# One block of linear attention on one core: where queries of the second token tile meet the first tile, and how a column of 2048 numbers is written

## The chip, the core and the metric

The kernel runs on one NeuronCore of a Trainium2 chip. Five engines work side by side and wait for each other through semaphores: TensorE (PE in the rows, with its weight loads as PEld), VectorE (DVE), ScalarE (ACT), GpSimd (POOL) and SyncE (SP), which issues most transfers. The metric is device time in microseconds; lower is better.

## The reference, cut to what matters

One transformer block for 256 tokens of width 2048, with 256 context tokens. Everything is float32. Two branches (window attention and a gated linear recurrence, "hgrn") are merged and projected. The change touches the recurrence, for each of 16 heads in both directions, and the output gate:

```
f = lbf + (1.0 - lbf) * jax.nn.sigmoid(z)          # forget gate; k = 1 - f
S_new = exp(G_end)[..., None] * S + einsum('bhsk,bhsv->bhkv', k * exp(G_end - G), v)
o     = einsum('bhtk,bhkv->bhtv', q * exp(G), S) + (the same chunk's keys, causal)
...
shift, scale, gate = jnp.split(silu(c) @ w_ada + b_ada, 3)
h = h + gate * merge_and_project(...)
```

A query therefore sees all earlier tokens either one by one, as keys and values with the decay between, or summed up in a state of 128 x 128 per head and direction.

## The kernel before, in words

The time goes into projections: 2048 x 19456 weights, streamed from HBM as `raw`, split by ACT (`wh`, L76) and by DVE (`wl`, L77) into two parts, and multiplied in three passes (L83, L84, L85). One chunk of weights is 24 matmuls of 512 columns; `wh` and `wl` have three buffers each, so ACT refills one as soon as the last matmul that reads it ends, three chunks ahead of its use.

The recurrence runs in eight steps, two heads each (`pair`, numbered here first to eighth). The order of PE's instructions is written out by hand: `pair` is a generator that issues some work and yields a number, and `weave` then lets that many units (1 unit = one chunk of 24 x 512 columns) of the next pair's projections (`inputs`) be issued before it goes on. The order on DVE and ACT is not written by hand; a scheduler sets it when the kernel is built, with the steps L76 and L77 at a higher priority.

A pair holds keys and queries of both directions in `A` (keys in A[0] and A[3], queries in A[2] and A[1]), the state from the context in `S` (a part of the tile `so`), and 256 tokens as two tiles of 128. It builds the products of queries and keys within a tile level by level (blocks of 1, 2, 4 to 64 tokens, `level`, L562, into the banks `al`); `grow` (L616) multiplies decays into `A` after each level; `keep` and `spread` copy the products into `AT`, the first half of the tile `X2` (printed `X` in the rows), through the piece `near` of its second half. Then three steps end a pair:

- four products across the two tiles, queries of the later against keys of the earlier (L677, L678, bank `a5`), which ACT copies into the second half of `AT` (L682); `grow(128)` multiplies the other tile's total decay into the queries (L610, L613);
- 1.5 units of filler;
- the outputs `ob`: for each tile and head four matmuls, own tile (L694), other tile (L696), and the two states (L697, L698).

Another generator, `gates`, sums up the output gate beside all this, on DVE, in four groups. `gate_end` turns a group with four PE transposes (`tqg`, L202), DVE reduces it (L204) and adds it into the column `gcol` (L206). After the fourth group POOL issues one transfer that writes `gcol`, 128 partitions of 16 numbers, to HBM in the order of 16 rows of 128 (L778); it is read back near the end. Next in POOL's order are the transfers of the bias rows `bb` (L465).

Of the kernel before, what the change touches and what calls it, by code (L numbers as in the profile page):

```python
# [7 lines left out]
F32 = mybir.dt.float32  # L8
F32R = mybir.dt.float32r
U8 = mybir.dt.uint8  # L10
AF = mybir.ActivationFunctionType
ALU = mybir.AluOpType
PSUM = bass.MemoryType.PSUM

P = 128
D = 2048
T = 256
KT = D // P
HD = 128
# [19 lines left out]
def block_kernel(ctx: ExitStack, tc: tile.TileContext, x, c, cx, c_ctx, w_ada, b_ada, norm_gain, w_in,  # L39
                 b_merge, lb_f, lb_b, hg_gain, w_oh, sink, w_oa, w_out, fin_gain, cst, msk, out):  # L40
    nc = tc.nc
    pe, act, dve, pool = nc.tensor, nc.scalar, nc.vector, nc.gpsimd

    def pl(name, bufs=1, **kw):
        return tc.tile_pool(name=name, bufs=bufs, **kw)
# [5 lines left out]
    base = ctx.enter_context(pl("base"))  # L51
    wp = ctx.enter_context(pl("wp"))
    pj = ctx.enter_context(pl("pj", 4, space=PSUM))
    ps = ctx.enter_context(pl("ps", 1, space=PSUM))
# [106 lines left out]
    ident = cs[:, K_ID: K_ID + P]  # L161
# [26 lines left out]
    def gate_chunk(acc, g, k0):  # L188

        wr = wload(w_ada, k0 * P, 2, (4096 + 512 * g,), 512)[1][:, 0]  # L190
        for j in range(2):
            cc = cg[:, k0 + j: k0 + j + 1]
            if k0 + j == 0:
                dve.tensor_scalar(acc, wr[:, j, :], cc, None, op0=ALU.mult)
            else:
                dve.scalar_tensor_tensor(acc, wr[:, j, :], cc, acc, op0=ALU.mult, op1=ALU.add)
# [20 lines left out]
    gcol = few.tile([P, KT], F32, name="gcol")  # L217
    gate_rows = dram.tile([KT, P], F32, name="gate_rows")

    FIRST = (("F0", 2), ("F1", 1), ("F0", 2))  # L220
    with pl("st", reuse_waits="tile") as st:
# [12 lines left out]
        with tc.high_priority(3 * PRIO):  # L234
# [8 lines left out]
            tp = ps.tile([P, 512], F32, tag="tp", name="tp")  # L243
# [11 lines left out]
        tp = ps.tile([P, 512], F32, tag="tp", name="tp")  # L255
# [220 lines left out]
    def pair(g, p, grp, F, banks_q):  # L476

        h0 = 4 * g + 2 * p
        v, vc, _ = grp

        A = hp.tile([P, 4, 512], F32, tag="A", name="A")
        X2 = hp.tile([P, 2048], F32, tag="X2", name="X2")
# [3 lines left out]
        Kmt = hp.tile([P, 2, 512], F32, tag="Km", name="Kmt")  # L486

        def v3(ap):
            return ap.rearrange("p (h t) -> p h t", h=2)
# [56 lines left out]
        def level(al, c0, b):  # L546

            n = 64 if b == 64 else 32
            for a in range(4):
                for g in range(4):  # L550
                    s0 = a * P + 32 * g
                    t0 = a * P + (32 * (g ^ 1) if b == 32 else 64 * (1 - g // 2) if b == 64 else 32 * g)
                    o = al[32 * g: 32 * g + 32, c0 + a * n: c0 + a * n + n]
                    if b == 0:
                        ky, mv = ksum[:, s0: s0 + 32], qT[:, t0: t0 + 32]
                    elif b in qslot:
                        ky, mv = cut(kslot[b], s0, 32), cut(qslot[b], t0, n)
                    else:
                        ky = cut(kslot[b], s0, 32)
                        o = o.rearrange("p (n two b) -> p n two b", two=2, b=b)  # L560
                        mv = mix(1, 1, t0, n, b)
                    pe.matmul(o, ky, mv, start=True, stop=True, tile_position=(0, 32 * g))  # L562

        def keep(al, c0, b):

            if b == 64:
                for c in range(2):
                    hf = slice(64 * c, 64 * c + 64)
                    act.activation(AT[hf, 0:4, 64 * (1 - c): 64 * (2 - c)],
                                   al[hf, c0: c0 + 256].rearrange("p (a b) -> p a b", a=4), AF.Copy)  # L570
# [8 lines left out]
        def spread():  # L579
            for g in range(4):  # L580
                rows = slice(32 * g, 32 * g + 32)
                for z in range(2):
                    c0 = 32 * (g ^ z)
                    act.activation(AT[rows, 0:4, c0: c0 + 32], near[rows, :, 32 * z: 32 * z + 32], AF.Copy)

        tots = {}

        def grow(b):

            n2 = 512 // (2 * b)  # L590
            if b == 1:
                even = [F[d][:, :, 0:T].rearrange("p h (n two) -> p h n two", two=2)[:, :, :, 0] for d in range(2)]
                odd = [F[d][:, :, 0:T].rearrange("p h (n two) -> p h n two", two=2)[:, :, :, 1] for d in range(2)]
            else:
                tv = tots[b].rearrange("p d (n two) -> p d n two", two=2)
                even, odd = tv[:, :, :, 0], tv[:, :, :, 1]
            toff = 1024 - 2 * 512 // b
            Tn = TT[:, toff: toff + 2 * n2].rearrange("p (d n) -> p d n", d=2)
            if b == 1:
                for d in range(2):  # L600
                    for a, par, f in ((d, 0, odd[d]), (2 + d, 1, even[d])):
                        av = v3(A[:, a, :]).rearrange("p h (n two) -> p h n two", two=2)[:, :, :, par]
                        dve.tensor_tensor(av, av, f, op=ALU.mult)
                    dve.tensor_tensor(v3(Tn[:, d, :]), even[d], odd[d], op=ALU.mult)
            else:
                for a0, par, f in ((0, 0, odd), (2, 1, even)):
                    av = A[:, a0: a0 + 2, :].rearrange("p a (n two b) -> p a n two b", two=2, b=b)[:, :, :, par, :]
                    if b == 128 and a0 == 0:

                        dve.tensor_tensor(av[:, 1], av[:, 1], f[:, 1].unsqueeze(2).to_broadcast([P, n2, b]),  # L610
                                          op=ALU.mult)
                    elif b == 128:
                        dve.tensor_tensor(av[:, 0], av[:, 0], f[:, 0].unsqueeze(2).to_broadcast([P, n2, b]),  # L613
                                          op=ALU.mult)
                    else:
                        dve.tensor_tensor(av, av, f.unsqueeze(3).to_broadcast([P, 2, n2, b]), op=ALU.mult)  # L616
                if b < 128:
                    dve.tensor_tensor(Tn, even, odd, op=ALU.mult)
            tots[2 * b] = Tn

        AT = X2[:, :1024].rearrange("p (a t) -> p a t", a=8)

        near = X2[:, 512:768].rearrange("p (a b) -> p a b", a=4)
        TT = X2[:, 1024:]
# [21 lines left out]
        S = so[:, 0, :].rearrange("p (d h v) -> p d h v", d=2, h=2)  # L646
        sb = ps.tile([P, 512], F32, tag="o", name="sb")
        for d in range(2):
            for i in range(2):
                o = sb[:, (2 * d + i) * HD: (2 * d + i + 1) * HD]  # L650
                for s in range(2):
                    pe.matmul(o, wT[:, 4 * d + 2 * i + s, :], vc[:, s, (2 * p + i) * HD: (2 * p + i + 1) * HD],  # L652
                              start=s == 0, stop=s == 1)
        act.activation(so[:, 0, :], sb, AF.Copy, scale=-1.0)

        grow(1)
        copies(2)
        grow(2)
        copies(4)
        yield 1.5  # L660
# [3 lines left out]
        for b in (4, 8, 16, 32):  # L664
            grow(b)
            copies(2 * b)
# [4 lines left out]
        a3, a4 = al_bank(), al_bank()  # L671
        for al, c0, b in ((a3, 0, 8), (a3, P, 16), (a3, 2 * P, 32), (a4, 0, 64)):
            level(al, c0, b)
        a5 = ps.tile([P, 512], F32, tag="o", name="al")
        for i in range(2):
            t0, t1 = slice(i * T, i * T + P), slice(i * T + P, (i + 1) * T)
            pe.matmul(a5[:, 2 * i * P: (2 * i + 1) * P], A[:, 0, t0], A[:, 2, t1], start=True, stop=True)  # L677
            pe.matmul(a5[:, (2 * i + 1) * P: (2 * i + 2) * P], A[:, 3, t1], A[:, 1, t0], start=True, stop=True)  # L678
        for al, c0, b in ((a3, 0, 8), (a3, P, 16), (a3, 2 * P, 32), (a4, 0, 64)):
            keep(al, c0, b)  # L680
        spread()
        act.activation(AT[:, 4:8, :], a5.rearrange("p (a b) -> p a b", a=4), AF.Copy)  # L682
        grow(128)
        yield 1.5


        ob = ps.tile([P, 2, 2, HD], F32, tag="o", name="ob")
        for t in range(2):
            tq = slice(t * P, (t + 1) * P)
            for i in range(2):  # L690
                o = ob[:, t, i, :]
                hv = slice((2 * p + i) * HD, (2 * p + i + 1) * HD)
                ht = slice(i * T + t * P, i * T + (t + 1) * P)
                pe.matmul(o, AT[:, 2 * i + t, :], v[:, t, hv], start=True, stop=False)  # L694

                pe.matmul(o, AT[:, 4 + 2 * i + (1 - t), :], v[:, 1 - t, hv], start=False, stop=False)  # L696
                pe.matmul(o, A[:, 2, ht], S[:, 0, i, :], start=False, stop=False)  # L697
                pe.matmul(o, A[:, 1, ht], S[:, 1, i, :], start=False, stop=True)  # L698
        srs = few.tile([P, 8], F32, tag="ss", name="ss", bufs=2)
        ss, rs = srs[:, :4], srs[:, 4:]  # L700
        ot = so[:, 1, :].rearrange("p (t h v) -> p t h v", t=2, h=2)
# [4 lines left out]
        for t in range(2):  # L706
            for i in range(2):
                dve.scalar_tensor_tensor(ot[:, t, i, :], ob[:, t, i, :], rs[:, 2 * t + i: 2 * t + i + 1],
                                         grp[2][:, t, (2 * p + i) * HD: (2 * p + i + 1) * HD],
                                         op0=ALU.mult, op1=ALU.mult)  # L710
# [59 lines left out]
    def gates():  # L770

        for g in range(4):
            for k0 in range(0, KT, 2):
                gate_chunk(accT[:, 0, :], g, k0)
                yield
            gate_end(accT[:, 0, :], g)

        nc.gpsimd.dma_start(gate_rows.rearrange("k p -> p k"), gcol)  # L778
        while True:
            yield  # L780

# [312 lines left out]
    for k0 in range(0, KT, 4):  # L1094
        h, lo = wchunk(w_out, k0 * P, 4, D - 512, 256)
# [15 lines left out]
    for t in range(2):  # L1111
# [7 lines left out]
        for c0, c1, on_act in ((0, 512, True), (512, 1024, False), (1024, 1536, True), (1536, D, False)):  # L1119
# [3 lines left out]
            else:  # L1123
                e = min(c1, D - 256)
                dve.tensor_scalar(xv[t][:, c0: e], xv[t][:, c0: e], rs, None, op0=ALU.mult)
                if e < c1:
                    dve.scalar_tensor_tensor(xv[t][:, e: c1], xv[t][:, e: c1], rs, fg[1][:, e - 1024: c1 - 1024],
                                             op0=ALU.mult, op1=ALU.mult)
# [54 lines left out]
```

## Time and profile before

| what | value |
|---|---|
| three timed runs | 1647.79, 1649.04, 1650.03 us; median 1649.04 us |
| the profiled execution | 1650.36 us, of which 1648.6 us from the first to the last instruction |
| PE busy | 1621.8 us, 98% of the span |
| DVE, ACT, POOL busy | 57%, 46%, 2% |
| TensorE's granted clock, mean | 0.994 |

The profile gives for each instruction its start, its length and what ended the idle time before it; matmuls overlap, so the distance between starts, not the length of one, is what PE pays for each.

### The profile page before, as it was taken

What the parts mean: (1) busy time and instruction counts of PE and PEld (TensorE: products, weight loads), DVE (VectorE), ACT (ScalarE), POOL (GpSimd) and SP (SyncE); (2) the same over time, 40 slices, a digit from 0 to 9 for tenths busy, and PEclk for the clock granted to TensorE, in tenths of its full rate; (3) what the DMA queues carried; (4) which work ended last, traced back from release to release, by engine and by line L of the source; (5) the groups of instructions that cost most, each with busy time, mean ns of one, the idle gap of its engine ahead of it and who ended that gap; (6) DMA issues with size and microseconds to landing.
All of it is one profiled execution on the core that took longest, in us unless ns stands there. A gap on an engine that the chain in (4) does not pass through costs nothing.

```text
span 1648.6 us, 24835 instructions
## 1 busy us (share of the span) xinstructions
PE 1621.8 (98%) x9913; PEld 1336.3 (81%) x9913; DVE 934.4 (57%) x1447; ACT 763.4 (46%) x1199; POOL 31.9 (2%) x88
## 2 busy tenths in 40 slices
PE   7999999999999999999899999999999999999998
PEld 4558888888888888888788888888888888788887
DVE  4444567546664466645457555334677676555665
ACT  4333454424543345424356443223576777444443
POOL 2000000000000000000000000000000000000000
PEclk9999999999999999999899999999999999999999
DMA  9993444346333553436335566424545455666564
GB/s 354 381 386 107 142 150 144 103 134 189 103 125 124 163 162 103 142 102 192 90 106 170 178 197 193 142 90 139 172 136 153 140 161 154 228 207 188 186 191 141
DMA packets 191443, 274.90 MB, mean 167 GB/s; under 512 B 9808, under 2 KB 112608, under 8 KB 190560
## 3 DMA queue, kind: packets, MB, share of 16 engines
q1 hardware_dynamic: 189344, 268.95, 51.4%
q0 software_dynamic: 1264, 3.25, 0.9%
q8 instruction: 78, 1.28, 0.3%
q10 hardware_dynamic: 720, 1.11, 0.2%
q14 instruction: 37, 0.30, 0.1%
HBM read 271.17 MB, written 2.11 MB: 166 GB/s over the span
## 4 chain that ended last, share of the span: by engine, by line
PE 94%; DMA 4%; DVE 1%; issue 1%; ACT 0%; SPq 0%; POOLq 0%; POOL 0%; ACTq 0%
PE pj L83 23%; PE pj L85 23%; PE pj L84 23%; PE pj L141 7%; PE pj L146 3%; DMA raw<-in_w_ada_dram 3%; PE al L562 1%; PE pa L306 1%; PE sb L652 1%; PE tkp L991 1%; DMA X<-in_ctx_dram 1%; PE pj L396 1%; PE pj L389 0%; PE oba L83 0%; PE ob L694 0%
## 5 line engine op out<-in xcount | busy, mean ns | idle before, releaser
L77 DVE TENSOR_TENSOR wl<-raw,wh 128x1024 fp32r<-128x1024 f32 x392 | 479.5, 1224 | 445.2 <-ACT wh L76 444.9
L76 ACT ACTIVATE wh<-raw 128x1024 fp32r<-128x1024 f32 x392 | 414.8, 1058 | 589.0 <-PE pj L85 426.0
L84 PE MATMUL pj<-wl,xHL 128*128 128x512 f32 (+1 forms) x1024 | 395.8, 387 | 0.4 <-DVE wl L77 0.4
L85 PE MATMUL pj<-wh,xHL 128*128 128x512 f32 (+1 forms) x1024 | 395.6, 387 | 0.0
L83 PE MATMUL pj<-wh,xHL 128*128 128x512 f32 (+1 forms) x1024 | 391.3, 390 | 0.0
L85 PEld LDWEIGHTS pj<-wh,xHL 128*128 128x128 f32 x1024 | 192.4, 188 | 39.0
L84 PEld LDWEIGHTS pj<-wl,xHL 128*128 128x128 f32 x1024 | 192.5, 188 | 38.3 <-DVE wl L77 0.7
L83 PEld LDWEIGHTS pj<-wh,xHL 128*128 128x128 f32 x1024 | 192.2, 188 | 38.0 <-DVE yt L1047 0.4
L141 PE MATMUL pj<-xHL,wh 128*128 128x512 f32 x512 | 180.9, 397 | 0.0
L83 PE MATMUL pj<-xHL,wh 128*128 128x512 f32 x416 | 165.6, 398 | 0.0
L85 PE MATMUL pj<-xHL,wl 128*128 128x512 f32 x416 | 163.1, 392 | 0.0
L84 PE MATMUL pj<-xHL,wh 128*128 128x512 f32 x416 | 163.0, 392 | 0.0
L146 PE MATMUL pj<-xHL,wl 128*128 128x256 f32 x512 | 139.4, 282 | 0.0
L141 PEld LDWEIGHTS pj<-xHL,wh 128*128 128x128 f32 x512 | 95.1, 188 | 19.5
L84 PE MATMUL pj<-wl,bH 128*128 128x512 f32 x256 | 100.0, 391 | 0.0
L85 PE MATMUL pj<-wh,bL 128*128 128x512 f32 x256 | 99.7, 390 | 0.0
L146 PEld LDWEIGHTS pj<-xHL,wl 128*128 128x128 f32 x512 | 96.6, 189 | 2.5
L85 PEld LDWEIGHTS pj<-xHL,wl 128*128 128x128 f32 x416 | 78.6, 189 | 16.7
L83 PEld LDWEIGHTS pj<-xHL,wh 128*128 128x128 f32 x416 | 78.8, 189 | 15.7
L84 PEld LDWEIGHTS pj<-xHL,wh 128*128 128x128 f32 x416 | 78.8, 189 | 15.7
L83 PE MATMUL pj<-wh,bH 128*128 128x512 f32 x256 | 89.9, 390 | 0.1
L616 DVE TENSOR_TENSOR A<-A,X 128x512 f32<-128x512 f32 x96 | 62.0, 687 | 23.0 <-ACT qk L538 6.7
(274 smaller groups left out, 1707.2 us busy)
## 6 DMA issues: line engine op xcount, KB each, us to landing
raw<-in_w_in_dram SPq DMA_DIRECT2D x292, 512.0 KB, 3.6
raw<-in_w_ada_dram SPq DMA_DIRECT2D x128, 256.0 KB, 5.4
raw<-in_w_ada_dram SPq DMA_DIRECT2D x32, 512.0 KB, 3.9
raw<-in_w_o_hgrn_dram SPq DMA_DIRECT2D x32, 512.0 KB, 3.6
raw<-in_w_o_attn_dram SPq DMA_DIRECT2D x32, 512.0 KB, 3.9
raw<-in_w_out_dram SPq DMA_DIRECT2D x32, 512.0 KB, 4.1
raw<-in_w_in_dram SPq DMA_DIRECT2D x24, 256.0 KB, 5.4
X<-in_x_dram SPq DMA_DIRECT2D x2, 1024.0 KB, 6.4
```

The lines of the kernel that those rows point to most:

```text
L76: act.activation(h[:, :n], raw[:, :n], AF.Copy)
L77: dve.tensor_tensor(lo[:, :n], raw[:, :n], h[:, :n].bitcast(F32), op=ALU.subtract)
L83: pe.matmul(o, s[0], m[0], start=first, stop=False)
L84: pe.matmul(o, s[0], m[1], start=False, stop=False)
L85: pe.matmul(o, s[1], m[0], start=False, stop=last)
L141: pe.matmul(banks[i].rearrange("p (a t) -> p a t", a=2), h[:, j, cs_], xHL[:, :, kt, :T], start=kt == 0, stop=kt == KT - 1)
L146: pe.matmul(banks[i][:, :T], lo[:, j, cs_], xH[:, kt, :T], start=False, stop=False)
L306: pe.matmul(pa[32 * g: 32 * g + 32, : 2 * w], cT[:, k0 + g, :], rv_[:, :, g % nk, :], start=k0 == 0, stop=k0 == KT - 4, tile_position=(0, ...
L396: pe.matmul(o, hw, xL[:, kt, :], start=False, stop=kt == KT - 1)
L562: pe.matmul(o, ky, mv, start=True, stop=True, tile_position=(0, 32 * g))
L616: dve.tensor_tensor(av, av, f.unsqueeze(3).to_broadcast([P, 2, n2, b]), op=ALU.mult)
L652: pe.matmul(o, wT[:, 4 * d + 2 * i + s, :], vc[:, s, (2 * p + i) * HD: (2 * p + i + 1) * HD], start=s == 0, stop=s == 1)
```

## The change

The four products across the tiles, their copy and `grow(128)` go. In their place the keys of each direction's first tile (tile 0 forwards, tile 1 backwards) are turned by four PE transposes (`kt`), copied by ACT into `KT` (a part of `Kmt`), and multiplied with that tile's values (`own`, one of the two `al` banks, by turns). DVE then makes `S2` = total decay x `S` + `own` in four steps, in the second half of `X2`, and the direction's second tile uses `S2` as its state. An output has three matmuls in place of four. The yield of 1.5 units is cut in two of 0.75, with the products `own` between.

```diff
-                if b < 128:
-                    dve.tensor_tensor(Tn, even, odd, op=ALU.mult)
+                dve.tensor_tensor(Tn, even, odd, op=ALU.mult)
...
-        a5 = ps.tile([P, 512], F32, tag="o", name="al")
-        for i in range(2):
-            t0, t1 = slice(i * T, i * T + P), slice(i * T + P, (i + 1) * T)
-            pe.matmul(a5[:, 2 * i * P: (2 * i + 1) * P], A[:, 0, t0], A[:, 2, t1], start=True, stop=True)
-            pe.matmul(a5[:, (2 * i + 1) * P: (2 * i + 2) * P], A[:, 3, t1], A[:, 1, t0], start=True, stop=True)
+        kt = ps.tile([P, 512], F32, tag="o", name="kt")
+        for d in range(2):
+            for i in range(2):
+                pe.transpose(kt[:, (2 * d + i) * P: (2 * d + i + 1) * P], A[:, 3 * d, i * T + d * P: i * T + (d + 1) * P],
+                             ident)
+        KT = Kmt[:, 0, :]
+        act.activation(KT, kt, AF.Copy)
...
         spread()
-        act.activation(AT[:, 4:8, :], a5.rearrange("p (a b) -> p a b", a=4), AF.Copy)
-        grow(128)
-        yield 1.5
+        yield 0.75
+        S2 = X2[:, 512:1024].rearrange("p (d h v) -> p d h v", d=2, h=2)
+        own = al_bank()
+        for d in range(2):
+            for i in range(2):
+                c0 = (2 * d + i) * HD
+                pe.matmul(own[:, c0: c0 + HD], KT[:, c0: c0 + HD], v[:, d, (2 * p + i) * HD: (2 * p + i + 1) * HD],
+                          start=True, stop=True)
+        for d in range(2):
+            for i in range(2):
+                c0 = (2 * d + i) * HD
+                dve.scalar_tensor_tensor(S2[:, d, i, :], S[:, d, i, :], tots[128][:, d, 2 * i + d: 2 * i + d + 1],
+                                         own[:, c0: c0 + HD], op0=ALU.mult, op1=ALU.add)
+        yield 0.75
...
-                pe.matmul(o, AT[:, 4 + 2 * i + (1 - t), :], v[:, 1 - t, hv], start=False, stop=False)
-                pe.matmul(o, A[:, 2, ht], S[:, 0, i, :], start=False, stop=False)
-                pe.matmul(o, A[:, 1, ht], S[:, 1, i, :], start=False, stop=True)
+                pe.matmul(o, A[:, 2, ht], (S2 if t else S)[:, 0, i, :], start=False, stop=False)
+                pe.matmul(o, A[:, 1, ht], (S if t else S2)[:, 1, i, :], start=False, stop=True)
...
-        nc.gpsimd.dma_start(gate_rows.rearrange("k p -> p k"), gcol)
+        tg = ps.tile([P, 512], F32, tag="tp", name="tgr")
+        pe.transpose(tg[:KT, :P], gcol, ident)
+        grow_ = base.tile([P, 512], F32, tag="sm", name="grow", bufs=3)
+        act.activation(grow_[:KT, :P], tg[:KT, :P], AF.Copy)
+        nc.gpsimd.dma_start(gate_rows, grow_[:KT, :P])
```

In the pieces of the instruction order below, a wait is given by the engine whose semaphore is waited for. The first place is PE at the end of the fourth pair (`so` holds `S`, the tile `X_` and a number holds `AT` and, after the change, `S2`). Before, the last two matmuls of the filler and the first outputs:

```order
L84 MATMUL pj<-xHL,wh 128x512
L85 MATMUL pj<-xHL,wl 128x512
L694 MATMUL ob<-v,X_4038 128x128 [waits Activation_49]
L696 MATMUL ob<-v,X_4038 128x128 [waits DVE_49]
L697 MATMUL ob<-so,A 128x128
L698 MATMUL ob<-so,A 128x128 [waits DVE_49]
```

The same place after the change:

```order
L84 MATMUL pj<-xHL,wh 128x512
L85 MATMUL pj<-xHL,wl 128x512
L684 MATMUL al<-v,Kmt 128x128 [waits DVE_49,Activation_49]
L684 MATMUL al<-v,Kmt 128x128 x3
L701 MATMUL ob<-v,X_4047 128x128 [waits PE_49,Activation_49]
L702 MATMUL ob<-so,A 128x128
L703 MATMUL ob<-X_4047,A 128x128 [waits DVE_49]
L701 MATMUL ob<-v,X_4047 128x128
L702 MATMUL ob<-so,A 128x128
L703 MATMUL ob<-X_4047,A 128x128 [waits DVE_49]
```

One chunk of 24 matmuls stands between the transposes and `own` (as it stood between `a5` and `ob`), and none between `own` and `ob`: the third matmul of the outputs reads what DVE makes of `own`. It is so in the first seven pairs; in the eighth 12 matmuls of filler stand between them.

The second place is DVE at the same end of the fourth pair. Before, from the last copies of the levels to the next pair's first step:

```order
L577 COPY_PREDICATED X_4038<-mk,al 128x4x32 [waits DVE_49]
L613 TENSOR_TENSOR A<-A,X_4038 128x2x128 [waits PE_49]
L610 TENSOR_TENSOR A<-A,X_4038 128x2x128 [waits PE_49]
L212 TENSOR_SCALAR F_4070<-sg,lbc 128x512 [waits Activation_49]
L77 TENSOR_TENSOR wl<-raw,wh 128x1024 [waits DMAHW6_49,PE_49,Activation_49]
L212 TENSOR_SCALAR F_4070<-sg,lbc 128x512 [waits Activation_49]
```

After the change:

```order
L577 COPY_PREDICATED X_4047<-mk,al 128x4x32 [waits DVE_49]
L212 TENSOR_SCALAR F_4079<-sg,lbc 128x512 [waits Activation_49]
L689 SCALAR_TENSOR_TENSOR X_4047<-so,X_4047,al 128x128 [waits DVE_49,PE_49]
L77 TENSOR_TENSOR wl<-raw,wh 128x1024 [waits DMAHW6_49,Activation_49]
L689 SCALAR_TENSOR_TENSOR X_4047<-so,X_4047,al 128x128 x3
L212 TENSOR_SCALAR F_4079<-sg,lbc 128x512 [waits Activation_49]
```

The first of the four steps for `S2` waits for PE; the other three stand behind a step `wl`, which waits for ACT's `wh`. The first seven pairs have this order; in the eighth all four stand together.

The third place is PE at the end of the gate's fourth group, after the change (before, the row of `tgr` is not there):

```order
L85 MATMUL pj<-xHL,wl 128x512
L202 MATMUL tqg<-cs,acc 128x128 [waits DVE_49,PE_49]
L202 MATMUL tqg<-cs,acc 128x128 x3
L784 MATMUL tgr<-cs,gcol 16x128 [waits DVE_49,PE_49]
L83 MATMUL pj<-xHL,wh 128x512
```

On DVE the order there is the same before and after, L204, a step `wl` (L77), then L206, whose result `tgr` reads; so PE's filler now stands behind L206.

## Rows read from the trace of the kernel before

**Rows 1.** The page: busy time by engine, and the chain by engine

```profile
PE 1621.8 (98%) x9913; PEld 1336.3 (81%) x9913; DVE 934.4 (57%) x1447; ACT 763.4 (46%) x1199; POOL 31.9 (2%) x88
...
PE 94%; DMA 4%; DVE 1%; issue 1%; ACT 0%; SPq 0%; POOLq 0%; POOL 0%; ACTq 0%
```

**Rows 2.** Waits, two stretches: waiting instruction, releaser, total us, times, longest us

```profile
PE idle L410 <- DVE cols L257: 2.4, 1, 2.4
...
PE al L562 <- issue: 6.1, 3, 2.8
```

**Rows 3.** Timeline of PE, end of the fourth pair: start, length, instruction

```profile
498.41 0.49 PE L677 MATMUL al<-A 128*128 128x128 f32 x2
...
499.33 0.47 PE L83 MATMUL pj<-xHL,wh 128*128 128x512 f32 x1
...
504.90 0.38 PE L694 MATMUL ob<-v,X 128*128 128x128 f32 x2
...
508.38 0.48 PE L83 MATMUL pj<-wh,xHL 128*128 128x512 f32 x1
```

**Rows 4.** Chain around the gate's transfer and in the sixth pair: start, length, what

```profile
801.91 0.44 PE tqg L202 x4
...
807.84 1.14 PE al L562 x73
...
835.70 1.46 PE al L562 x98
...
676.46 1.23 PE al L562 x82
...
694.25 1.46 PE al L562 x98
```

**Rows 5.** Timeline of DVE, end of the fourth pair

```profile
505.96 1.23 DVE L77 TENSOR_TENSOR wl<-raw,wh 128x1024 fp32r<-128x1024 f32 x1 [1.79 <-ACT wh L76]
507.10 0.54 DVE L212 TENSOR_SCALAR F<-sg,lbc 128x512 f32<-128x512 f32 x1
...
512.36 1.12 DVE L708 SCALAR_TENSOR_TENSOR so<-ob,ss,gate 128x128 f32<-128x128 f32 x4
```

**Rows 6.** Timeline of ACT, ends of the fourth and of the third pair

```profile
504.87 1.06 ACT L76 ACTIVATE wh<-raw 128x1024 fp32r<-128x1024 f32 x1 [1.28 <-PE pj L84]
...
508.67 0.28 ACT L704 ACTIVATE so<-ob 128x128 f32<-128x128 f32 x1 [2.25 <-PE ob L698]
...
439.74 1.06 ACT L76 ACTIVATE wh<-raw 128x1024 fp32r<-128x1024 f32 x1
```

**Rows 7.** Chain in the third pair: its first outputs

```profile
439.28 0.49 PE ob L694 x2
```

**Rows 8.** Timelines of PE and DVE: a restart of PE behind a wait

```profile
1441.35 0.50 PE L84 MATMUL pj<-wl,xHL 128*128 128x512 f32 x1 [0.42 <-DVE wl L77]
1441.69 0.40 PE L85 MATMUL pj<-wh,xHL 128*128 128x512 f32 x1
...
1440.07 1.23 DVE L77 TENSOR_TENSOR wl<-raw,wh 128x1024 fp32r<-128x1024 f32 x1 [2.63 <-ACT wh L76]
```

**Rows 9.** Timelines of DVE and POOL at the gate's end

```profile
802.38 0.69 DVE L204 TENSOR_REDUCE redg<-tqg 128x4 f32<-128x512 f32 x1 [2.32 <-PE tqg L202]
...
804.13 0.16 DVE L206 TENSOR_TENSOR gcol<-redg,gcol 128x4 f32<-128x4 f32 x1
...
804.58 1.26 POOL L778 DMA_DIRECT2D gate_rows<-gcol  x1 [95.93 <-DVE gcol L206]
```

**Rows 10.** Transfers of bias rows, 800 to 822 us and all: count, size, median us to landing

```profile
bb<-in_b_merge_dram POOLq DMA_DIRECT2D x2, 256.0 KB, 13.7
...
bb<-in_b_merge_dram POOLq DMA_DIRECT2D x8, 256.0 KB, 4.8
```

**Rows 11.** Windows: stretch, its length, busy us (instructions) of each engine, PEclk, DMA share, GB/s

```profile
816.60:821.60 5.00, 5.00 (x19) 3.90 (x13) 3.40 (x7) 2.07 (x5) 0.00 (x0) 0.50 0.64 181
...
19.70:26.50 6.80, 5.95 (x28) 3.54 (x32) 0.97 (x4) 0.00 (x0) 0.00 (x0) 0.50 1.09 384
```

More of the change, by code (lines that the diff above doesn't have):

```diff
@@ L607, in grow @@
                     av = A[:, a0: a0 + 2, :].rearrange("p a (n two b) -> p a n two b", two=2, b=b)[:, :, :, par, :]
[L608 to L616, printed above, removed]
-                if b < 128:
-                    dve.tensor_tensor(Tn, even, odd, op=ALU.mult)
+                    dve.tensor_tensor(av, av, f.unsqueeze(3).to_broadcast([P, 2, n2, b]), op=ALU.mult)
+                dve.tensor_tensor(Tn, even, odd, op=ALU.mult)
             tots[2 * b] = Tn
-        AT = X2[:, :1024].rearrange("p (a t) -> p a t", a=8)
+        AT = X2[:, :512].rearrange("p (a t) -> p a t", a=4)
         near = X2[:, 512:768].rearrange("p (a b) -> p a b", a=4)
```

## The prediction

> **What bounds the kernel now.** I began with the page: PE is busy for 98% of the span and makes 94% of the chain that ended last [rows 1]. So an edit counts by what it takes from or adds to PE's own stream, and by each time it lets PE stand still; what DVE and ACT gain or lose is free as long as PE does not wait for it. Then I read PE's waits. Behind the start-up the only long ones are three stops of 6.1 us in all inside the level products of the seventh pair, which end for no reason that the profile shows [rows 2]. The chain tells what that place costs. From the first level products of a pair to its second group the sixth pair takes 694.25 - 676.46 = 17.79 us, the seventh 835.70 - 807.84 = 27.86 us [rows 4], for the same work. That is 10.07 us too much: the stops themselves, and a stretch behind them in which the granted clock is 0.50, the lower of its two levels (1.2 against 2.4 GHz) [rows 11]. The stops begin some 5 us after POOL issued the gate's transfer at 804.58 [rows 9], and the two bias transfers queued right behind it needed 13.7 us to land, where the median of all eight is 4.8 [rows 10].
>
> **PE's own work.** A 128x128 product in float32 is two instructions in the rows. The four across the tiles took 499.33 - 498.41 = 0.92 us, and the 16 of the outputs 508.38 - 504.90 = 3.48 us, so 0.22 each [rows 3]. Gone are 0.92 + 4 x 0.22 = 1.80 us a pair. New are four products at 0.22 = 0.88 and four transposes, which at the gate took 0.44 together [rows 4]; sum 1.32. That is 0.48 us saved a pair, 3.8 us over eight. On ACT one copy of 128x512 takes the place of another; on DVE two steps go and four come, all beside PE's filler except as follows.
>
> **The new wait.** Before, a chunk of filler lay between the last thing that DVE or ACT had to make and `ob`. Now the chunk lies between `kt` and `own`, and `ob` follows `own` at once in seven pairs, so PE meets a round trip through DVE with no cover. I count from the start of `own` (which is where `ob` started before, 504.90).
> - PE: `own` 0.88, then two of the first three output products, 0.44: at 1.32 PE needs the third step of `S2`.
> - DVE: its first step of `S2` waits for PE. ACT's first reader of a finished bank started 508.67 - 508.38 = 0.29 us behind the next matmul's start [rows 3, 6]; the readers of one bank wait for its last product, so DVE starts at 0.88 + 0.2 = about 1.1. Four such steps on a bank take 1.12 us, 0.28 each [rows 5], so it is free at 1.37.
> - The `wl` behind it needs `wh`, which ACT can only start when the last chunk gives its buffer back: 504.87, 1.06 long, so at 1.03 [rows 6]. It holds DVE for 507.10 - 505.96 = 1.14 us [rows 5], to 2.51. Two more steps of `S2`: 3.07.
> - PE starts 0.05 us behind DVE's end (1440.07 + 1.23 against 1441.35) and its first step then takes 0.34 us where the steady one takes 0.23, 0.1 more [rows 8]. So PE goes on at 3.12, 1.8 us late, and the wait costs 1.9 us.
>
> In the third pair `wh` starts 0.46 us behind `ob` and not just ahead of it [rows 6, 7], so `wl` starts at 1.55, 0.18 later: 2.1 us. In the eighth 12 matmuls of filler (2.7 us) cover the four steps, which there stand together: nothing. Sum 6 x 1.9 + 2.1 = 13.5 us. From below it is 1.5 us a pair (DVE's first step done before `wh`, so that `wl` runs from 1.06; no restart), 10.5 in all; from above 2.2 us a pair, 15.4. PE's later chunks are split well ahead, so nothing behind the wait runs short; the second half of the forget gate (L212) stands last on DVE and its reader comes much later.
>
> **The gate's column.** `tgr` stands on PE right behind `tqg` and needs L206, which ends at 804.13 + 0.16 = 804.29 [rows 9], with L204 and a `wl` ahead of it. PE was done with `tqg` at 802.35 by the chain [rows 4], with the next matmul issued up to 0.25 us before that. So it stands for 2.0 to 2.2 us, plus the restart and the transpose itself, 0.1 each: 2.3 us, between 1.0 (no `wl` ahead) and 2.5. Then POOL's transfer has 16 runs of 512 bytes in place of 2048 of 4. If the 2048 small writes are what stopped PE, the 10.07 us come back; from below it is nothing, if they were not. I take the whole, because no other pair with the same products shows such a stop, and other bias transfers run without one.
>
> The page "DMA: Bandwidth & Descriptors" of the Trainium skill speaks against this: in "Queues, rings and completion order" it says that each transfer engine takes its queues in turn, packet by packet, so that a queue with little work should not wait long behind a full one. By it the small writes could not hold up anything of PE's for several microseconds, the stops would have another cause, and the sum would be that of the second rival below. No row shows what PE waited for; the slow landing behind the gate's transfer is on the same queue and bears on neither.
>
> **The sum.** -3.8 + 13.5 + 2.3 - 10.1 = +1.9 us. Against the profiled execution's 1650.36 that is 1652.3; against the median of the runs, 1649.04, it is 1650.9 us, which I give. The bounds of the waits (10.5 + 1.0 and 15.4 + 2.5) make it -2.4 to +4.0: 1646.6 to 1653.0. A difference within 0.2% (3.3 us) is about what a measurement of this kernel cannot tell from none.
>
> **The rivals.**
> - *The clock falls at the new waits* (slower). After the 2.4 us wait near the start [rows 2] the granted clock was 0.50 from 19.7 to 26.5 us, and after the stops in the seventh pair too [rows 11]; after the 0.42 us wait [rows 8] it stayed. The new waits of 1.9 to 2.3 us lie near the upper end. Against it: dense matmuls stand on both sides of them. In 5 us at 0.50 PE does half of its work, so a fall costs some 2.5 us; in three of eight places it is +7.5, 1658.4; in all eight +20, 1671. It decides from two falls on.
> - *The stops stay* (slower). They come from the code of the level products or from the bias transfers, which stay. For it: nothing in the rows names their releaser. Then -3.8 + 13.5 + 2.3 = +12.0: 1661. It is also the case where the second half of the change does not do what it should.
> - *The wait for `S2` is short* (faster). If DVE has three steps of `S2` done before `wl` gets its `wh`, PE waits for 1.1 + 3 x 0.28 + 0.05 - 1.32 = 0.7 us, 0.8 with the restart; seven are 5.6 in place of 13.5, the sum -6.0, 1643. The order on DVE speaks against it, since three steps stand behind `wl`. It decides below 1.2 us a pair.
>
> **How the numbers follow.** The forecast has 0.58: it lies within 0.2% for 0.42, beyond it slower for 0.15, faster for 0.01. The clock has 0.15 and the stops 0.10, both slower; the short wait 0.14, faster; 0.03 is left, which I share out. So faster 0.16, same 0.43, slower 0.41. The range 1645.5 to 1661 holds the forecast's bounds, most of the clock's case up to four falls and the case of the stops, and leaves out the short wait and many falls, about 0.2.
>
> **What would show it.** In the profile after: PE idle before L703 for some 1.8 us, seven times, put down to DVE's L689, and in the eighth pair not; `wl` between the first and second L689; one wait of about 2 us before L784, put down to L206; no wait of "issue" in the seventh pair's L562, some 17.8 us between its two groups, no stretch at clock 0.50 behind the start; the next bias transfers landing in some 5 us. Wrong would be: a granted clock of 0.50 behind the waits, or the stops still there.

## The result, and the profile after

The changed kernel takes 1652.96 us (median of 10 runs, 1652.41 to 1654.4) against 1649.03 us (10 runs): +3.93 us, a ratio of 1.0026 with a 95% interval of 1.0016 to 1.0035. It is slightly slower, inside the forecast range and 2.1 us above the forecast of 1650.9. By the prediction's own line of 0.2% it counts as slower, which had a chance of 0.41, and not as the same, which had 0.43; the interval reaches across that line. The profiled execution took 1652.92 us, with a span of 1651.1.

PE's waits in the whole span, waiting instruction, releaser, total us, times, longest us:

```profile
PE ob L703 <- DVE X L689: 11.7, 7, 1.8
...
PE tgr L784 <- DVE gcol L206: 2.1, 1, 2.1
```

The three stops of [rows 2] are gone and two waits are new: seven before the third matmul of the outputs, one before the transpose of the gate's column. The end of the fourth pair, which [rows 3] show for before, on PE (timeline: start, length, instruction, idle time before it and what ended it):

```profile
503.78 0.38 PE L669 MATMUL kt<-cs,A 128*128 128x128 f32 x2
...
509.48 1.05 PE L684 MATMUL al<-v,Kmt 128*128 128x128 f32 x8
510.36 0.39 PE L701 MATMUL ob<-v,X 128*128 128x128 f32 x2
510.59 0.39 PE L702 MATMUL ob<-so,A 128*128 128x128 f32 x2
512.62 0.49 PE L703 MATMUL ob<-X,A 128*128 128x128 f32 x2 [1.64 <-DVE X L689]
```

The same on DVE and, last, ACT's `wh`:

```profile
510.57 0.35 DVE L689 SCALAR_TENSOR_TENSOR X<-so,X,al 128x128 f32<-128x128 f32 x1 [1.36 <-PE al L684]
510.83 1.22 DVE L77 TENSOR_TENSOR wl<-raw,wh 128x1024 fp32r<-128x1024 f32 x1
511.96 0.86 DVE L689 SCALAR_TENSOR_TENSOR X<-so,X,al 128x128 f32<-128x128 f32 x3
...
509.45 1.06 ACT L76 ACTIVATE wh<-raw 128x1024 fp32r<-128x1024 f32 x1 [0.82 <-PE pj L84]
```

From the start of `own` (509.48) the prediction had DVE's first step at 1.1, `wl` at 1.37, the other three from 2.51, PE at 3.12. They came at 1.09, 1.35, 2.48 and 3.14. Counted between starts, as the prediction counts, PE is 1.81 us late: L703 was due at 510.59 + 0.22 and started at 512.62. The profile's idle time says 1.64, because it counts from the modelled end of the matmul before. The outputs then run on as before.

At the gate, PE and DVE:

```profile
811.18 0.60 PE L202 MATMUL tqg<-cs,acc 128*128 128x128 f32 x4
813.86 0.27 PE L784 MATMUL tgr<-cs,gcol 128*16 128x128 f32 x1 [2.08 <-DVE gcol L206]
...
812.43 1.21 DVE L77 TENSOR_TENSOR wl<-raw,wh 128x1024 fp32r<-128x1024 f32 x1
813.56 0.15 DVE L206 TENSOR_TENSOR gcol<-redg,gcol 128x4 f32<-128x4 f32 x1
```

Here too a `wl` stands between the sum's two steps, and PE stands still for 2.1 us. The chain through the two groups of level products of the seventh pair, and the transfers at that place (count, size, us to landing), answer to [rows 4] and [rows 10]:

```profile
819.62 1.23 PE al L562 x82
837.37 1.50 PE al L562 x98
...
gate_rows<-grow POOLq DMA_DIRECT2D x1, 8.0 KB, 2.5
...
bb<-in_b_merge_dram POOLq DMA_DIRECT2D x2, 256.0 KB, 3.7
```

The two groups are 17.75 us apart in place of 27.86, and the bias transfers land in 3.7 us in place of 13.7. Between the start-up and the last 5 us of the span the granted clock shows no stretch at 0.50; before had one at its end too.

### The profile page after: what moved, and what is told of

Its sections match the earlier page's. It is cut to its first block, busy times and chain, and to the rows that moved or that the text cites. A ratio compares the mean times of both kernels' runs of the same rounds, so it can differ in the third digit from the quotient of the medians.

```text
span 1651.1 us, 24815 instructions
## 1 busy us (share of the span) xinstructions
PE 1616.8 (98%) x9882; PEld 1330.1 (81%) x9882; DVE 937.2 (57%) x1463; ACT 763.7 (46%) x1200; POOL 31.6 (2%) x88
## 4 chain that ended last, share of the span: by engine, by line
PE 91%; DMA 4%; DVE 3%; ACT 1%; issue 1%; POOLq 0%; POOL 0%; SPq 0%; ACTq 0%; DVEq 0%
PE pj L83 23%; PE pj L84 23%; PE pj L85 23%; PE pj L141 7%; PE pj L146 3%; DMA raw<-in_w_ada_dram 3%; DVE wl L77 1%; PE al L562 1%; PE pa L306 1%; PE sb L643 1%; PE tkp L1000 1%; PE pj L396 1%; PE pj L389 1%; PE pj L390 1%; PE oba L83 0%
## 5 line engine op out<-in xcount | busy, mean ns | idle before, releaser
L77 DVE TENSOR_TENSOR wl<-raw,wh 128x1024 fp32r<-128x1024 f32 x392 | 479.1, 1223 | 428.1 <-ACT wh L76 427.7
L141 PEld LDWEIGHTS pj<-xHL,wh 128*128 128x128 f32 x512 | 95.1, 188 | 19.7
L196 DVE SCALAR_TENSOR_TENSOR acc<-raw,cg,acc 128x512 f32<-128x512 f32 x60 | 44.9, 749 | 47.9 <-DMA raw<-in_w_ada_dram 47.4
```

Source lines behind the costliest of these rows:

```text
L77: dve.tensor_tensor(lo[:, :n], raw[:, :n], h[:, :n].bitcast(F32), op=ALU.subtract)
L141: pe.matmul(banks[i].rearrange("p (a t) -> p a t", a=2), h[:, j, cs_], xHL[:, :, kt, :T], start=kt == 0, stop=kt == KT - 1)
```

## The experiments

All times are medians of device time. Twelve kernels ran, in four sessions; the kernel before had medians of 1648.2 to 1648.9 us in these. The ratios are against before in the same session; a difference between two other kernels is one of medians, in part across sessions, and can be off by some 0.8 us for that alone.

**The rows alone** (before, with only the gate's write changed):

```diff
-        nc.gpsimd.dma_start(gate_rows.rearrange("k p -> p k"), gcol)
+        pe.transpose(tg[:KT, :P], gcol, ident)
+        act.activation(grow_[:KT, :P], tg[:KT, :P], AF.Copy)
+        nc.gpsimd.dma_start(gate_rows, grow_[:KT, :P])
```

> The kernel before with the gate column written as 16 rows, and nothing else changed. My account: the stops in the seventh pair go (10.1 us back) and PE waits about 2.1 us before the transpose of the column (2.3 us with the transpose and the restart): -7.8 us, about 1641. Rival (the stops come from the code of the level products or from the bias transfers, which are still there): +2.3 us, about 1651, with the waits of 'issue' still in the seventh pair.

1642.54 us, ratio 0.9967 (0.9954 to 0.9979). No wait of "issue" behind the start-up is left; PE has one long wait:

```profile
PE tgr L779 <- DVE gcol L206: 2.1, 1, 2.1
```

So the stops hung on the 2048 small writes; the code of the level products and the bias transfers are the same in this kernel. It gained 5.8 us where 7.8 were expected.

**The states alone** (the changed kernel with the old write of the column, the edit above turned round):

> The changed kernel with the gate column written as before (2048 writes of 4 bytes). My account: PE's products give 3.8 us and the seven waits for S2 take 13.5: +9.7 us, about 1659, with the stops in the seventh pair as before. Rival (the stops hang on the old products across the tiles, not on the write): the stops are gone and the time is that of the changed kernel or less.

1659.08 us, ratio 1.0066 (1.0052 to 1.008). Both waits are there:

```profile
PE ob L703 <- DVE X L689: 11.6, 7, 1.7
...
PE al L562 <- issue: 4.7, 2, 3.6
```

The half of the change that the title names first costs 10.8 us by itself; the rows give 6.1 us of it back (1659.08 - 1652.96).

**A chunk between `own` and the outputs:**

```diff
                                          own[:, c0: c0 + HD], op0=ALU.mult, op1=ALU.add)
-        yield 0.75
+        yield 1.25
```

> The changed kernel with the second yield of 0.75 made 1.25, so that one chunk of filler stands between the products own and the outputs in the first seven pairs. My account: no wait before L703, 13.5 us less than the changed kernel, about 1639.5. Rival (PE's stream itself is dearer, or DVE is so far behind that a chunk does not cover it): the wait moves to another place, 1648 or more.

1640.11 us, ratio 0.9946 (0.9934 to 0.9959), 12.9 us less than the changed kernel. Its five runs lie in two groups (1638.2 and 1638.5; 1640.1 to 1640.8), so this difference is known to some 2 us. PE no longer waits before L703 and no new wait appears; the filler that fills the gap is work that PE does later in any case.

**The four sums ahead of `wl`:**

```diff
-                dve.scalar_tensor_tensor(S2[:, d, i, :], ...)
+                with tc.high_priority(2 * PRIO):
+                    dve.scalar_tensor_tensor(S2[:, d, i, :], ...)
```

> The changed kernel with a higher priority for the four steps of S2, so that the scheduler puts all four ahead of the step wl on DVE. My account: the wait before L703 falls from 1.8 to 0.7 us (1.1 until the first step, three steps of 0.28, 0.05, less the 1.32 that PE has to do), 7.7 us less than the changed kernel, about 1645, unless the later wl stops PE elsewhere. Rival (the round trip between the engines is the cost, and wl only stands beside it): within 2 us of the changed kernel, 1651 to 1653.

1643.88 us, ratio 0.9976 (0.9966 to 0.9985), 9.1 us less than the changed kernel. The waits on PE and, at the fourth pair, DVE's four sums in one piece with `wl` behind them:

```profile
PE ob L704 <- DVE X L690: 3.6, 7, 0.5
...
505.98 1.12 DVE L690 SCALAR_TENSOR_TENSOR X<-so,X,al 128x128 f32<-128x128 f32 x4 [1.29 <-PE al L684]
507.02 1.22 DVE L77 TENSOR_TENSOR wl<-raw,wh 128x1024 fp32r<-128x1024 f32 x1
```

Of 11.7 us of waits 3.6 are left: about two thirds of the price was the place of one step on DVE, not the round trip. The later `wl` stops nothing.

**The transpose of the column later, and both covers.** In `gates`, one more `yield` ahead of the transpose; the second kernel has the chunk as well.

```diff
+        yield
         tg = ps.tile([P, 512], F32, tag="tp", name="tgr")
```

> The changed kernel with one more yield in the gate's generator, so that some 16 us of filler stand between the fourth group's sum and the transpose of the column. My account: no wait before the transpose, 2.2 us less than the changed kernel, about 1650.7. Rival (the wait only moves, since the transpose lands among the level products): the same time as the changed kernel, 1653.

> The changed kernel with both covers: the chunk of filler between own and the outputs, and the later transpose of the column. My account: neither wait is left, 1639.5 less 2.2, about 1637.5. Rival (the two covers take filler from each other): 1640 or more.

1650.86 us (ratio 1.0015, 1.0006 to 1.0024), 2.1 us less than the changed kernel: the wait goes and does not come back elsewhere. With both covers 1636.28 us, ratio 0.9927 (0.9914 to 0.9939), the fastest kernel here, 12.1 us below before in its session. PE's longest wait behind the start-up is now 0.4 us.

**The column's small writes, later.** First only with one or two more yields ahead of the old transfer:

> The kernel before with one more yield ahead of the gate's transfer (2048 writes of 4 bytes as before), which then starts some 16 us later, between the two groups of level products of the seventh pair. If the small writes stop PE where its code runs fast: the stops leave the first group and come in the second or at the pair's end, and the time stays about 1649. If the stops hang on the code of the first group or on the bias transfers: they stay where they were. If they hang on the writes but need the first group: gone, about 1639.

> The kernel before with two more yields ahead of the gate's transfer, which then starts some 32 us later, behind the seventh pair's last outputs, where only projections run for some 20 us. If the small writes stop PE only where its code runs fast (level products, 32 columns each): no stop, or a short one, about 1639 to 1642. If they stop it anywhere: a stop of several us among the projections, about 1649.

These told nothing apart: 1648.81 us (0.9991 to 1.0009) and 1649.14 us (0.9996 to 1.0014). The yields order PE alone; the transfer needs only `gcol`, and POOL issued it at 804.0 and 804.5 us, as before. They show the same stops twice more: 6.3 and 4.4 us of "issue" among the level products, and stretches at a clock of 0.50, in and behind them, of different length:

```profile
812.80:819.60 6.80, 4.54 (x26) 3.59 (x27) 3.14 (x7) 1.43 (x3) 0.00 (x0) 0.50 0.50 97
...
814.00:817.40 3.40, 3.40 (x19) 2.72 (x17) 2.12 (x5) 1.10 (x3) 0.00 (x0) 0.50 0.28 10
```

(Windows of the one and of the other: stretch, length, busy times, PEclk, DMA share, GB/s.) Then with a copy of the column through PE and ACT, which POOL must wait for, still written as 2048 numbers:

```diff
-        nc.gpsimd.dma_start(gate_rows.rearrange("k p -> p k"), gcol)
+        yield
+        pe.matmul(tg[:, :KT], ident, gcol, start=True, stop=True)
+        act.activation(gc2[:, :KT], tg[:, :KT], AF.Copy)
+        nc.gpsimd.dma_start(gate_rows.rearrange("k p -> p k"), gc2[:, :KT])
```

> The kernel before, with the gate column copied once more through PE and ACT one step of the gate's generator later (some 16 us), and written from the copy, still as 2048 writes of 4 bytes. Unlike a yield alone this moves the transfer, since POOL must wait for the copy; it starts just ahead of the second group of level products of the seventh pair. If the small writes stop PE where its code runs fast: no stop in the first group, stops in the second; time about 1649. If the stops hang on the first group's code or on the bias transfers: they stay there. If they need the first group together with the writes: gone, about 1639.

> The same with the copy two steps later, so that the transfer starts behind the seventh pair's last outputs, where some 27 us of projections follow. If the small writes stop PE only where its code runs fast: no stop or one under 2 us, about 1639 to 1641. If they stop it anywhere: several us of 'issue' among the projections, about 1649.

One step later (issued at 822.6): 1642.63 us, 0.9966 (0.9953 to 0.9978). Two steps later (844.2): 1641.28 us, 0.9956 (0.9942 to 0.9969). What is left of the stops, and the transfer, first one step later, then two:

```profile
PE al L562 <- issue: 1.0, 2, 0.6
...
gate_rows<-gc POOLq DMA_DIRECT2D x1, 8.0 KB, 15.2
...
gate_rows<-gc POOLq DMA_DIRECT2D x1, 8.0 KB, 16.7
```

In the first the stops left the first group of level products and came, far smaller, in the second; in the second there are none of "issue" on PE, though 8 KB still took 16.7 us to land. So the writes are slow wherever they stand, and in the six profiles with them no stop of "issue" came anywhere but among level products. A time of 1649 was expected of the first; it was 6 us better, because the stop is short there and the clock does not fall.

Why the stop is so short there stays open, for these two kernels moved something else too. POOL no longer issues the bias transfers right behind the small writes (before: 804.58 and 806.93) but some 15 and 37 us ahead of them; one step later:

```profile
807.55 1.20 POOL L465 DMA_DIRECT2D bb<-in_b_merge_dram  x2 [0.21 <-POOL bb L464]
...
822.59 1.20 POOL L783 DMA_DIRECT2D gate_rows<-gc  x1 [13.85 <-ACT gc L782]
```

That the long stops need the bias transfers queued behind the small writes is a rival that no run here separates.

One thing does not hang on that order. The weights (`raw`), which SyncE issues on a queue of its own, landed late beside the small writes wherever these stood (before, 808 to 816.5 us; changed kernel, 814 to 830; two steps later, 844 to 860):

```profile
raw<-in_w_in_dram SPq DMA_DIRECT2D x1, 512.0 KB, 12.6
...
raw<-in_w_in_dram SPq DMA_DIRECT2D x3, 512.0 KB, 3.5
...
raw<-in_w_in_dram SPq DMA_DIRECT2D x4, 512.0 KB, 12.6
```

PE's waits show none for these weights.

**The rows with the transpose later** (before, with the rows and the extra `yield`, without the states):

> The kernel before with the gate column written as 16 rows and the transpose one step of the generator later; the products across the tiles are those of before. My account: no stops and no wait for the transpose, 2.2 us less than the kernel with the rows alone (1642.5): 1640.3. Against it the kernel with both covers (1636.3), which has the states too, tells what the states are worth without a wait: 3.8 us by my account; rival (the states save nothing on PE): the two within 1 us.

1640.37 us, ratio 0.9951 (0.9938 to 0.9965). Against it the kernel with both covers is 4.1 us faster, or 3.6 if each is first compared with before in its own session: that is what the states are worth once nothing waits for them.

**A longer wait** (the rows alone, with two idle steps of DVE ahead of the transpose):

```diff
+        with tc.high_priority(2 * PRIO):
+            dve.tensor_tensor(gw.rearrange("p (a k) -> p a k", k=KT), gcol..., gcol..., op=ALU.max)
+            dve.tensor_tensor(gw, gw, gw, op=ALU.max)
-        pe.transpose(tg[:KT, :P], gcol, ident)
+        pe.transpose(tg[:KT, :P], gw[:, :KT], ident)
```

> The kernel before with the gate column written as 16 rows, and two steps of DVE of 0.6 us each added between the sum and the transpose, so that PE's one wait there grows from 2.1 to about 3.3 us. The rival of the prediction in which the clock falls at a wait: a stretch at a granted clock of 0.50 behind this wait in the profile, and more than the 1.2 us of the longer wait added to the kernel with the rows alone (1642.5): 1645.4 or more in most runs. My account (a wait of this size costs its own length): 1643.7, no such stretch.

1645.72 us, ratio 0.9985 (0.9976 to 0.9994), 3.2 us more than the rows alone, with all 11 runs between 1645.3 and 1646.5. PE before and behind the wait, and a window behind it:

```profile
805.71 0.37 PE L784 MATMUL tgr<-cs,gw 128*16 128x128 f32 x1 [3.53 <-DVE gw L782]
805.73 0.77 PE L83 MATMUL pj<-xHL,wh 128*128 128x512 f32 x1
806.30 0.63 PE L84 MATMUL pj<-xHL,wh 128*128 128x512 f32 x1
...
806.00:808.00 2.00, 2.00 (x6) 1.53 (x5) 0.00 (x0) 0.27 (x1) 0.58 (x1) 0.50 0.58 203
```

The wait is 3.5 us, 1.4 longer, and the clock then stands at 0.50 (matmuls of 0.63 us for 0.39) until 809 us. The rival is right for a wait of this size; the other 1.8 us go with the 3.4 us at the lower clock.

## Why the prediction was right, and what was off

- **PE's own work.** Forecast -3.8 us; the two kernels without waits differ by 3.6 to 4.1. Right.
- **The wait for `S2`.** Forecast 13.5 us. Right in place, count, cause and size: seven waits, none in the eighth pair, with a `wl` between the first and the other sums. Six have 1.64 to 1.65 us of idle time and the third pair's has 1.82, 0.17 more where the prediction had 0.18. Taking the wait away gave 12.9 us with the gate's wait still there, and 14.6 without (1650.86 - 1636.28). That the place of `wl` makes most of it is shown by the kernel with the four sums first: 0.5 us of idle time each, or about 0.7 with the 0.17 that the count between starts adds, which is what the rival of the short wait had worked out for that order.
- **The gate's transpose.** Forecast 2.3 us; moving the transpose away gave 2.1 (idle 2.1 in the trace).
- **The stops.** Forecast -10.1 us, all that the seventh pair had too much in the one trace of before. That they go with the small writes is shown: writing rows takes them away in both kernels, writing numbers brings them back. The size was off. The kernel with the rows and no waits is 8.6 us below before (1640.37 against 1648.94 in that session), not 10.1. The stretch at a clock of 0.50 around the stops is of different length in each profile, 10.2 us in that of before and 3.4 to 6.8 in the three others with the old write, and the profiled execution of before was one of the slower ones (1650.36 against a median of 1649.03). This term of the sum was sized from one execution; with 1.5 us it is the larger part of the 2.1 that were missed, and the wait for `S2` (1.1) comes next.
- **The sum.** With the measured terms: -4.1 + 14.6 + 2.1 - 8.6 = +4.0 us, against +3.93 measured. This does not confirm the terms: the four are the steps of one chain of kernels from before to the changed one, so they add up by themselves. The halves alone are the check. The states alone should give -4.1 + 14.6 = +10.5 and gave +10.8; the rows alone should give 2.1 - 8.6 = -6.5 and gave -5.8.
- **The rivals.** The clock did not fall at waits of 1.6 to 2.1 us in the profiled executions and did at 3.5, so that rival was near and not met there. Its own example does not bear on it: the clock fell at 19.7 us, inside the 2.4 us wait, which ends at 20.55, and PE had been busy for only 1.78 of the 3.4 us before. The stops did not stay. The short wait needs the sums ahead of `wl`; the scheduler had not put them there.
- **The page on transfers.** The Trainium skill's page "DMA: Bandwidth & Descriptors", section "Queues, rings and completion order", has the transfer engines take their queues in turn, packet by packet. From that the prediction inferred that the small writes should hold up nobody for long. The runs differ: PE stood for 4.4 to 6.3 us in the four profiles with the small writes in their old place, and not where rows are written. The prediction set the slow landing aside as one on the writes' own queue. That left out a row: in the same 800 to 822 us two weight transfers of SyncE's queue are listed at a median of 8.1 us, one at 3.5 and one, issued behind 808 us, at 12.6. The measurement decides that the writes bring the stops and hold up another queue. How they do it, and what PE lacked, no row shows. That it was code would fit stops among short instructions alone, but is not shown: the trace of before counts no packet of the kind "instruction" between 803 and 822 us, and PE went on at 816 without one.

## What to carry to other kernels

Where one engine is the bound, count its own work, and then for each new edge to another engine the work that stands between its two ends: here some 4 us of PE's work were saved and 13 to 15 lost for want of one chunk between a product and its reader, a change of one number. Look at what the scheduler puts into the round trip on the other engine; one step of 1.2 us with a higher priority, itself waiting for a third engine, made two thirds of the price. A wait "for nothing that the profile shows" is worth tracing to the transfers that run beside it, on all queues, and its price should be taken from several executions where the clock falls behind it.

## What was not expected of the hardware

- 8 KB written as 2048 numbers of 4 bytes took 12.3 to 16.7 us to land in the three profiles that record it; as 16 rows of 512 bytes it took 1.6 to 4.1 us. What stood behind the numbers on their queue landed in 13.7 us for 3.7, and weights on another queue in 12.6 for 3.5.
- The runs of kernels with waits of about 2 us on PE fall into two clusters: with the rows alone three at 1641.9 to 1642.5 and two at 1644.0 to 1644.1 us, while those of the kernels without such a wait lie close (1636.2 to 1636.4 and 1640.3 to 1640.9). The wait of 3.5 us, behind which the profile shows the fall of the clock, has one cluster again. That the clock falls at the shorter waits in some executions would explain it. No profile can tell, for each profiled execution of these kernels lies in the lower cluster (1642.54 us with the rows alone), so it stays open.
